# Conv layer norm of a streaming encoder: row sums kept in order of time, high parts written by silu, the output in blocks

## Chip, cores and metric

One NeuronCore of one Trainium2 chip runs the whole step. The metric is the device time of one execution in microseconds, median over runs. Five engines work side by side, each through its own queue in order: PE (matmuls; its weight loads are shown as PEld), DVE, ACT, POOL, and SP, which here only issues DMAs.

## The reference, cut to what matters

Two groups of frames (512 new ones and 64 of running streams, T = 576 columns in all) go through two layers of width 1024. The first layer mixes in time with a Conformer convolution, the second with attention; each is followed by a SwiGLU FFN, and one RMS norm ends the whole.

```python
def conv_module(xn, prefix, w_in, b_in, w_dw, b_dw, ln_g, ln_b, w_out, b_out):
    a, gate = jnp.split(xn @ w_in + b_in, 2, axis=-1)
    u = a * jax.nn.sigmoid(gate)
    u_ext = jnp.concatenate([prefix.astype(u.dtype), u], axis=1)
    y = lax.conv_general_dilated(u_ext, w_dw[:, None, :], ...) + b_dw   # 31 taps, each channel alone
    y = jax.nn.silu(layernorm(y, ln_g, ln_b))
    return y @ w_out + b_out, u_ext[:, -CONV_STATE:]
# trunk: h = h + conv_module(...); h = h + swiglu(rmsnorm(h)); h = h + attention; h = h + swiglu(...)
# return rmsnorm(h, final_norm_g), ...
```

## The kernel before

Activations lie transposed: 8 tiles c = 0..7 of 128 channels by T columns. Every fp32 operand of a product is split into a high part (rounded to fp32r by ACT) and a low part (what is left, by DVE or POOL), and one product is three matmuls: high weights with high activations, high with low, low with high (`mm_ops`, L578, helper line L592). A product of one output tile `wi`, one input tile k and both halves of T is six matmuls.

A planner (class `Plan`, L111) collects operations with a cost, the keys that they read and write, and a few flags. `flush` orders all operations of a section by list scheduling: an engine that comes free takes, among what the planner's own clock has ready, the operation with the longest way to the end (`urgent` ones first), and takes something of lower rank rather than idle. Each engine's queue gets that order. The planner knows the keys only. Waits that come from a new PSUM pool taking over the banks of an old one are not among them; they are added when tiles are placed.

**The convolution.** Tiles 4, 5 and 7 (`POLY`) are convolved on PE in four phases of time (`conv_phases`, L905; products on L923), tiles 0, 1, 2, 3 and 6 (`ROWS`) by taps on DVE (L1046) and on ACT with POOL (L1060, L1063). For the layer norm, sums over channels of y and of y squared are needed. For the row tiles `rows_sums` (L1086) adds each finished y to `ys`, and `square` (L1080) squares it on ACT and adds it to the squares of the first one. Both sums are kept in phases: `in_phases` (L1031) reads a row of time with a stride of four floats. After the last tile (6), `rows_stat` sends both over PE, which sums over partitions (`stat_rows`, L983, helper L979), into one accumulator `cl`. All those matmuls come behind the one that opens the accumulator, the sum `yes` of tiles 4 and 5 that POOL adds up (L1014 to L1026). `warm` matmuls (L775) fill PE's gaps.

**The seam.** From `cl` a short chain on ACT and DVE makes the negative mean `nmp` and the reciprocal deviation `rp`; PE spreads them over all partitions into PSUM (`spread_time`, L1179, helper L1186): `nm` (tag p0), `rt` (tags p5, p4), and a second copy of the mean, `nm2` (tag p1), which ACT copies to SBUF as `nms` for the two tiles that POOL centres. Each tile c is then centred (L1232: DVE reads `nm`; POOL for c = 5 and 7), multiplied by `rt` (L1240), put through silu in place (L1244), copied to its high part (L1250), and the low part is the difference (L1254; POOL for c = 1, 3, 5). Tile 0 goes by halves. Operations on an engine "next" stand for PE's use of the parts, so that the planner sees the order in which they are wanted.

The next section begins with the eight output tiles of w_out (`w_out_tile`, L1799), in the order 0, 4, 1, 5, ... PSUM is a new pool there, and its tags take the eight banks in order of first use: output tile i = 0 (b4, b5) the banks of the tap accumulator, i = 1 (b2, b3) those of p1, i = 2 (b0, b1) those of p0, that is of `nm`. Weights are split in units of 512 columns, two for each output tile. During the convolution four places (w0 to w3) hold the units of i = 0 and 1; the places w4 and w5 open with the next section.

**The end.** `tail` (L1733) finishes the last two output tiles by halves of T; for each half a Newton step (`newton_step`, L681) makes `r`, and the eight tiles of that half are scaled by it: tiles 1, 2, 4, 6 on POOL (`Y_POOL`, L1785; with a scaled copy of h by ACT, L1729), the others on DVE (L1787). Four DMAs of two tiles each (L1795) write that half of `yT`.

Of the kernel before, what the change touches and what calls it, by code (L numbers as in the profile page):

```python
# [75 lines left out]
Y_POOL = (1, 2, 4, 6)  # L76
# [18 lines left out]
WPOOL = {f"{q}{i}" for q in ("w", "wh", "wl") for i in range(4)} | {f"wr{i}" for i in range(3)}  # L95
N_S = 4
# [123 lines left out]
def build(tc, xT, vec, st, stp, bdp, wt, ck, cv, w_in, w_out, gu, down, wk, wv, wq, wo, yT, csp, css, kp, ks, vp, vs):  # L220
# [7 lines left out]
    kpool = ctx.enter_context(tc.tile_pool(name="kpool", bufs=1))  # L228
    dram = ctx.enter_context(tc.tile_pool(name="dram", bufs=1, space=bass.MemoryType.DRAM))
# [86 lines left out]
    def wide(tag):  # L316

        return wpool if tag in WPOOL else cur[0]

# [69 lines left out]
    free = {"wr": [], "w": ["w0", "w1", "w2", "w3"], "S": []}  # L389
# [9 lines left out]
    def place_for(q, ahead):  # L399

        for t in free[q]:
            if not ahead or t in WPOOL:
                free[q].remove(t)
                return t

    def advance():
# [9 lines left out]
        while pos["unit"] < len(units):  # L416
# [4 lines left out]
            tag = place_for("w", u >= eu)  # L421
# [127 lines left out]
    def section():  # L549

        pos["end"] += 1
        hbanks.clear()
        for q in free:
            free[q] = [t for t in free[q] if t in WPOOL]

# [22 lines left out]
    def mm_ops(dst, tag, wi, xkeys, start=True, stop=True, halves=(0, 1), xdeps=None, order=None, keep=False, apart=()):  # L578

        n = len(xkeys)  # L580
        for q, k in enumerate(order or range(n)):
            xk, u = xkeys[k], tile_units[wi][k // 4]

            def f(halves, k=k, xk=xk, u=u, q=q):
# [3 lines left out]
                for j in range(3):  # L588
                    for hf in halves:
# [4 lines left out]
                            start=(start and q == 0 and j == 0), stop=(stop and q == n - 1 and j == 2),  # L594
                        )

            for hs in [(hf,) for hf in halves] if k in apart else [halves]:
                deps = xdeps(xk) if xdeps else [xk + ("h",), xk + ("l",)]
                deps += [xk + (p, 1) for p in "hl"] if 1 in hs else []
# [4 lines left out]
                op("PE", 3 * len(hs) * pe(HA), lambda f=f, hs=hs: f(hs), reads=wkeys(u) + deps, writes=out, group=None if wi < 2 * NC else (wi, halves))  # L604
# [4 lines left out]
    class Norm:  # L609
# [27 lines left out]
        def rstd(self, pair, hf=None, urgent=False):  # L637
# [11 lines left out]
            root(key, tag, halves, rk, urgent)  # L649

    def root(key, tag, halves, rk, urgent=False, wide_=False):
# [27 lines left out]
        newton_step(r[:, sl], lambda: X[("rx",) + key][:, sl], n, xk, rk, urgent)  # L679

    def newton_step(y, x, n, xk, yk, urgent=False):  # L681
# [10 lines left out]

        op("DVE", dve(n), f, reads=yk[:1], writes=[xk], urgent=urgent, port=True)
# [1759 lines left out]
```

## Time and profile before

| | us |
|---|---|
| median of 3 runs (1233.16 to 1234.01) | 1234.01 |
| profiled execution | 1235.98 |
| its span, first to last instruction | 1234.2 |
| PE busy in the span | 1209.6 |
| DVE, ACT, POOL busy | 979.0, 979.4, 772.3 |

Times in the views are microseconds from the first instruction of the profiled execution. "Granted clock" is the share of TensorE's full 2.4 GHz that was granted; 0.50 is 1.2 GHz. In a timeline "x8" counts instructions merged into the row, and square brackets give idle time of that engine before the row and what ended it. An fp32 matmul shows as two records, an fp32r one as one.

### The profile page before, as it was taken

How to read it: one execution, taken by the hardware profiler on the slowest of the kernel's cores; microseconds unless marked ns; L12 is line 12 of the kernel's file. 1: busy time of each engine (PE TensorE's matmuls, PEld its weight loads, DVE VectorE, ACT ScalarE, POOL GpSimd, SP SyncE). 2: the span in 40 equal slices, each digit the busy share in tenths (PEclk: the TensorE clock that was granted, in tenths of full speed). 3: DMA queues.
4: the chain of work that ended last, by engine and by line, in shares of the span. 5: the costliest groups of instructions: out<-in, count | busy, mean ns of one | idle time of the engine just before them, and what ended most of it. 6: DMA issues, size and time to landing. Idle time of an engine off the chain costs nothing.

```text
span 1234.2 us, 24275 instructions
## 1 busy us (share of the span) xinstructions
PE 1209.6 (98%) x8950; PEld 1190.2 (96%) x8950; DVE 979.0 (79%) x1593; ACT 979.4 (79%) x1879; POOL 772.3 (63%) x640
## 2 busy tenths in 40 slices
PE   9999999999999999999999999998999999999996
PEld 8999989999999999999999999998999999999995
DVE  6999976967665669886688999999866666599965
ACT  7988464698887888687678999955988888896873
POOL 1999823479767757855215555554877768676732
PEclk9999989999999999999999999999999999999998
DMA  7333812133242333223372232232232232332222
GB/s 268 87 93 101 260 57 84 52 103 104 70 132 75 101 88 103 87 72 107 112 204 66 49 86 65 53 104 69 69 118 88 86 120 70 103 103 86 86 69 78
DMA packets 46023, 121.10 MB, mean 98 GB/s; under 512 B 8784, under 2 KB 16272, under 8 KB 45904
## 3 DMA queue, kind: packets, MB, share of 16 engines
q1 hardware_dynamic: 45904, 119.56, 32.3%
q8 instruction: 70, 1.15, 0.4%
q14 instruction: 49, 0.40, 0.1%
HBM read 105.18 MB, written 5.70 MB: 90 GB/s over the span
## 4 chain that ended last, share of the span: by engine, by line
PE 80%; DVE 8%; issue 2%; ACT 1%; POOL 0%; DMA 0%; SPq 0%; DVEq 0%; POOLq 0%; ACTq 0%
PE j_A L1411 29%; PE j_B L1411 14%; PE j_C L1411 7%; PE pd L592 7%; PE po L592 4%; PE pq L592 4%; PE b L2189 4%; PE pw L592 2%; PE b L2125 2%; PE b L2217 2%; DVE acc L1046 2%; PE pg L592 1%; PE pv L1940 1%; PE pk L592 1%; DVE wl L520 1%
## 5 line engine op out<-in xcount | busy, mean ns | idle before, releaser
L510 ACT ACTIVATE wh<-wr 128x512 fp32r<-128x512 f32 (+1 forms) x303 | 184.0, 613 | 40.1 <-PE po L592 17.2
L520 DVE TENSOR_TENSOR wl<-wr,hp 128x512 fp32r<-128x512 f32 (+1 forms) x241 | 158.8, 663 | 53.5 <-ACT hp L515 52.0
L520 DVE TENSOR_TENSOR wl<-S,hp 128x512 fp32r<-128x512 f32 x226 | 152.6, 682 | 41.8 <-ACT hp L515 39.0
L510 ACT ACTIVATE wh<-S 128x512 fp32r<-128x512 f32 x228 | 141.1, 626 | 32.6 <-PE pd L592 10.5
L515 ACT ACTIVATE hp<-wr 128x512 fp32r<-128x512 f32 (+1 forms) x241 | 138.9, 578 | 23.9 <-DVE wl L520 20.3
L515 ACT ACTIVATE hp<-S 128x512 fp32r<-128x512 f32 x226 | 133.7, 595 | 12.2 <-POOL S L440 7.1
L440 POOL TENSOR_TENSOR S<-wr,wr 128x512 f32<-128x512 f32 x57 | 76.3, 1338 | 94.6 <-ACT wh L510 38.0
L1063 POOL TENSOR_TENSOR pacc<-pacc,pr 128x608 f32<-128x608 f32 x69 | 109.0, 1595 | 7.3 <-ACT pr L1060 4.1
L476 POOL TENSOR_TENSOR S<-wr,S 128x512 f32<-128x512 f32 x57 | 78.1, 1371 | 31.3 <-DVE wl L520 17.2
L440 POOL TENSOR_TENSOR S<-wr 128x512 f32<-128x512 f32 x57 | 78.2, 1373 | 25.9 <-DVE wl L520 10.1
L440 POOL TENSOR_TENSOR S<-S,wr 128x512 f32<-128x512 f32 x57 | 78.5, 1377 | 12.1 <-DVE wl L520 5.8
L1588 POOL TENSOR_TENSOR a<-a,r 128x576 f32<-128x576 f32 x44 | 67.5, 1536 | 15.7 <-DVE a L1565 14.8
L1588 POOL TENSOR_TENSOR t<-t,r 128x576 f32<-128x576 f32 x44 | 66.5, 1515 | 10.0 <-ACT t L1559 8.7
L592 PE MATMUL pd<-ap,wh 128*128 128x288 f32 x384 | 66.0, 294 | 0.0
L1046 DVE SCALAR_TENSOR_TENSOR acc<-u,vecs,acc 128x608 f32<-128x608 f32 x76 | 64.7, 851 | 1.0
L1060 ACT ACTIVATE pr<-u,vecs 128x608 f32<-128x608 f32 x69 | 54.2, 798 | 8.2 <-POOL pacc L1063 7.9
L520 DVE TENSOR_TENSOR wl<-wr,wh 128x512 fp32r<-128x512 f32 x62 | 49.7, 813 | 7.8 <-ACT wh L510 7.7
L592 PEld LDWEIGHTS pd<-ap,wh 128*128 128x128 f32 x384 | 55.9, 188 | 0.0
L1594 DVE TENSOR_TENSOR a<-a,t 128x576 f32<-128x576 f32 x44 | 48.1, 1094 | 8.1 <-ACT t L1592 7.8
L1559 ACT ACTIVATE t<-j_A 128x288 f32<-128x288 f32 x84 | 34.0, 407 | 22.8 <-PE j_A L1411 22.2
L1680 DVE TENSOR_TENSOR h<-j_A,h 128x288 f32<-128x288 f32 x60 | 27.2, 455 | 19.6 <-PE j_A L1411 19.4
L1565 DVE TENSOR_TENSOR t<-j_C,t 128x288 f32<-128x288 f32 x42 | 19.2, 457 | 29.1 <-PE j_C L1411 28.8
(856 smaller groups left out, 4523.7 us busy)
## 6 DMA issues: line engine op xcount, KB each, us to landing
wr<-gu SPq DMA_DIRECT2D x88, 512.0 KB, 3.6
wr<-down SPq DMA_DIRECT2D x32, 512.0 KB, 4.1
wr<-w_in SPq DMA_DIRECT2D x15, 512.0 KB, 3.9
wm<-wt SPq DMA_DIRECT2D x12, 576.0 KB, 5.4
wr<-down SPq DMA_DIRECT2D x16, 384.0 KB, 3.1
qd<-qd SPq DMA_DIRECT2D x21, 256.0 KB, 3.2
wr<-w_out SPq DMA_DIRECT2D x8, 512.0 KB, 3.6
wr<-wq SPq DMA_DIRECT2D x8, 512.0 KB, 3.9
```

The costliest lines, as they stand in the source:

```text
L440: eng(e).tensor_tensor(t[:, :n], x[1](), y[1](), op=ALU.subtract if sub else ALU.add)
L476: eng(e).tensor_tensor(v[:, :n], X[("raw", i0)][:, n : 2 * n], v[:, :n], op=ALU.subtract)
L510: nc.scalar.activation(X[("w", u)][0][:, :n], get(), AF.Copy)
L515: nc.scalar.activation(t[:, :n], get(), AF.Copy)
L520: eng(le).tensor_tensor(b[:, :n], get(), a.bitcast(F32)[:, :n], op=ALU.subtract)
L592: nc.tensor.matmul(o[hf], (hi, hi, lo)[j][:, s], (xh, xl, xh)[j], start=(start and q == 0 and j == 0), stop=(stop and q == n - 1 and j == 2),)
L1046: nc.vector.scalar_tensor_tensor(dst, src, wt_, dst if i else X[("kneg",)], op0=ALU.mult, op1=ALU.add)
L1060: nc.scalar.activation(tile(("pr", c, i), f"pr{m}", (P, YW)), src, AF.Copy, scale=wt)
L1063: nc.gpsimd.tensor_tensor(X[("pacc", c)], X[("pacc", c)], X[("pr", c, i)], op=ALU.add)
L1411: nc.tensor.matmul(out, a[:, s], b, start=(start and q == 0 and i == 0), stop=(q == len(ops_) - 1 and i == 2), skip_group_check=True,)
L1588: nc.gpsimd.tensor_tensor(X[k], X[k], r, op=ALU.mult)
L2189: nc.tensor.matmul(zz()[:, a : a + n], X[("trir",) if same else ("oner",)], X[key][:, x, c : c + n], start=False, stop=(i == len(mms) - 1) ...
```

## The change

- `ys` and the squares are kept in order of time; PE now reads them with the stride of four floats (`stat_rows`). The sum of tiles 0 to 3 goes to PE after tile 3, and tile 6 goes to PE by itself instead of being added to `ys`.
- The square of tile 6 is made by halves, one on ACT and one on DVE.
- `nm2` is gone; ACT makes `nms` from `nm`, after tile 0 has been centred.
- silu writes the high part itself (rounded on output), and a second silu in place makes the full value from which the low part is taken. For the first three output tiles PE takes, for each input tile, the two matmuls with its high part and then the one with the low part of the tile before (`lag`).
- A fifth place w4 is open during the convolution, for the first unit of output tile i = 2 only.
- In the tail, `newton_step` also writes its result to a PSUM bank, and DVE's scalings read it there; POOL keeps tiles 2 and 4 only. `yT` has the shape (2, 4, 128, 576), so that each DMA writes one contiguous block; the host puts it back in order.

```diff
-Y_POOL = (1, 2, 4, 6)
+Y_POOL = (2, 4)
...
+WPOOL2 = {"w4", "wh4", "wl4"}
...
-    def place_for(q, ahead):
+    def place_for(q, ahead, third=False):
         for t in free[q]:
-            if not ahead or t in WPOOL:
+            if t in WPOOL or (third if t in WPOOL2 and not pos["end"] else not ahead):
...
-            tag = place_for("w", u >= eu)
+            tag = place_for("w", u >= eu, u >= eu + 4)
...
-        for q, k in enumerate(order or range(n)):
+        steps = [(q, k, (0, 1, 2)) for q, k in enumerate(order or range(n))]
+        if lag:
+            steps = [x for c in range(n + 1) for x in ((c, c, (0, 2)), (c - 1, c - 1, (1,))) if 0 <= x[0] < n]
+        for q, k, js in steps:
...
-                for j in range(3):
+                for j in js:
...
+        def b():
+            o = tile(("rb", bank), bank, (P, 512), pool=pp)[:, :n]
+            nc.vector.scalar_tensor_tensor(o, x(), 1.5, y, op0=ALU.add, op1=ALU.mult)
...
+        if bank:
+            op("DVE", dve(n, True), b, reads=[xk] + yk[:1], writes=[bank], urgent=urgent, port=True)
         op("DVE", dve(n, True), s, reads=[xk], writes=yk, urgent=urgent, port=True)
...
+            if q and c == ROWS[-1]:
+                nc.vector.tensor_tensor(o, x, x, op=ALU.mult)
+            else:
+                nc.scalar.activation(o, x, AF.Square)
...
+        if c == ROWS[-1]:
+            op("ACT", act(HY, False), lambda: f(0), reads=[("y", c)], writes=[(tag, 0)], urgent=True)
+            op("DVE", dve(YW - HY), lambda: f(1), reads=[("y", c)], writes=[(tag, 1)], urgent=True, port=True)
...
         if c in KN[2:]:
-            add(("ys",), "ys", ("y", c), ("y", c), True)
+            add(("ys",), "ys", ("y", c), ("y", c))
...
-            add(("ys",), "ys", ("y", c), ("y", c), True)
+            if c != ROWS[-1]:
+                add(("ys",), "ys", ("y", c), ("y", c))
             square(c)
...
-        stat_rows(lambda: X[("ys",)], "ys", 0)
-        stat_rows(lambda: X[("sq", a)], "ysq0", 1)
+        if c == ROWS[-2]:
+            stat_rows(lambda: in_phases(X[("ys",)]), ["ys"], 0)
+        if c == ROWS[-1]:
+            stat_rows(lambda: in_phases(X[("y", c)]), [("y", c)], 0)
+            stat_rows(lambda: in_phases(X[("sq", a)]), by_part("ysq0"), 1)
...
-    spread_time(("nm2",), "nmp", "p1")
-    op("ACT", act(T, False), lambda: nc.scalar.activation(tile(("nms",), "kneg", (P, YW))[:, :T], X[("nm2",)][:, O0 : O0 + T], AF.Copy), reads=both("p1"), writes=["kneg"])
...
-            nc.scalar.activation(part(X[("zt", c)][0], hs), part(X[("zf", c)], hs), AF.Copy)
+            nc.scalar.activation(part(X[("zt", c)][0], hs), part(X[("zf", c)], hs), AF.Silu, scale=col(V_LNG + c), bias=col(V_LNB + c))
...
+        if not c:
+            op("ACT", act(T, False), lambda: nc.scalar.activation(tile(("nms",), "kneg", (P, YW))[:, :T], X[("nm",)][:, O0 : O0 + T], AF.Copy), reads=NT + [zt], writes=["kneg"])
...
-            nrm.rstd(("b6", "b7"), hf, True)
+            nrm.rstd(("b6", "b7"), hf, True, ("b5", "b2")[hf])
...
-                            nc.vector.scalar_tensor_tensor(o, h[c][:, sl], col(V_FIN + c), r[:, sl], op0=ALU.mult, op1=ALU.mult)
+                            nc.vector.scalar_tensor_tensor(o, h[c][:, sl], col(V_FIN + c), X[rb][:, : sl.stop - sl.start], op0=ALU.mult, op1=ALU.mult)
...
-                    nc.sync.dma_start(yT[2 * q : 2 * q + 2, :, sl].rearrange("c p t -> p c t"), X[yk])
+                    nc.sync.dma_start(yT[hf, q], X[yk].rearrange("p c t -> p (c t)"))
...
+        if i < 3:
+            mm_ops(k, tag, wi, [("z", c) for c in range(NC)], apart=() if i else (0,), lag=True)
```

## Rows read from the trace of the kernel before

**Rows 1.** The page: busy time, share of the span and instructions of each engine.

```profile
PE 1209.6 (98%) x8950; PEld 1190.2 (96%) x8950; DVE 979.0 (79%) x1593; ACT 979.4 (79%) x1879; POOL 772.3 (63%) x640
```

**Rows 2.** Windows: stretch, length, busy per engine (instructions), granted clock, DMA share, GB/s.

```profile
160.00:170.00 10.00, 7.44 (x50) 6.74 (x49) 9.85 (x26) 7.88 (x13) 5.39 (x5) 0.84 0.17 52
...
300.00:500.00 200.00, 200.00 (x1510) 200.00 (x1509) 140.13 (x221) 167.01 (x341) 147.19 (x113) 1.00 0.32 95
...
168.00:170.00 2.00, 2.00 (x9) 2.00 (x10) 2.00 (x6) 1.45 (x3) 2.00 (x2) 0.50 0.00 0
...
174.00:176.00 2.00, 2.00 (x17) 2.00 (x16) 2.00 (x3) 1.97 (x5) 0.46 (x1) 1.00 0.00 0
```

**Rows 3.** Waits of PE from 110 to 180 us: total, times, longest.

```profile
PE po L592 <- POOL zl L1254: 2.0, 1, 2.0
...
PE po L592 <- ACT nms L1215: 0.5, 1, 0.5
```

**Rows 4.** Timeline of the seam: start, length, engine, line, operation, count, [idle before].

```profile
160.77 0.63 ACT L1244 ACTIVATE zf<-zf,vecs 128x288 f32<-128x288 f32 x1 [1.89 <-DVE zf L1240]
...
160.97 1.95 PE L1186 MATMUL nm<-nmp,row_of 128*128 128x72 f32 x16
...
162.72 0.38 PE L592 MATMUL po<-zh,wh 128*128 128x288 f32 x1
...
166.30 1.92 DVE L1232 TENSOR_TENSOR zf<-y,nm 128x512 f32<-128x512 f32 x4
...
167.90 0.85 PE L592 MATMUL po<-zl,wh 128*128 128x288 f32 x2 [1.99 <-POOL zl L1254]
```

**Rows 5.** ACT's silu and copy in the seam: shortest, median, longest in ns.

```profile
L1244 ACT ACTIVATE zf<-zf,vecs x9: 627/856/870, 160.8 to 173.4; 128x576 f32<-128x576 f32 x7, 128x288 f32<-128x288 f32 x2
...
L1250 ACT ACTIVATE zh<-zf x9: 444/667/689, 161.4 to 174.3; 128x576 fp32r<-128x576 f32 x7, 128x288 fp32r<-128x288 f32 x2
```

**Rows 6.** Timeline of DVE in the convolution: row sums, squares and a weight's low part.

```profile
75.27 2.00 DVE L1093 TENSOR_TENSOR ys<-y,y 128x608 f32<-128x608 f32 x1
...
86.05 1.75 DVE L1134 SCALAR_TENSOR_TENSOR ys<-kneg,ys 128x608 f32<-128x608 f32 x1
...
125.65 0.68 DVE L520 TENSOR_TENSOR wl<-wr,hp 128x512 fp32r<-128x512 f32 x1
...
132.02 2.56 DVE L1076 TENSOR_TENSOR ys<-ys,y 128x608 f32<-128x608 f32 x1
...
135.27 1.30 DVE L1076 TENSOR_TENSOR sq<-sq,sq 128x608 f32<-128x608 f32 x1
```

**Rows 7.** Timeline of the convolution's end: phase products, sums and the first reader.

```profile
141.96 7.25 PE L923 MATMUL py<-vt,wm 128*128 128x152 f32 x54 [0.51 <-DVE ye L933]
...
149.04 0.45 PE L979 MATMUL cl<-yes,sum_of 128*128 128x152 f32 x2
...
152.05 1.32 ACT L1082 ACTIVATE sq<-y 128x608 f32<-128x608 f32 x1 [0.60 <-DVE y L1070]
...
152.15 1.26 DVE L1076 TENSOR_TENSOR ys<-ys,y 128x608 f32<-128x608 f32 x1
...
153.40 0.79 DVE L1076 TENSOR_TENSOR sq<-sq,sq 128x608 f32<-128x608 f32 x1
...
154.61 1.20 PE L979 MATMUL cl<-sq,sum_to 128*128 128x152 f32 x8
...
155.84 0.30 ACT L1192 ACTIVATE vs<-cl 128x152 f32<-128x152 f32 x1 [2.48 <-PE cl L979]
```

**Rows 8.** Timeline of the last half of the output.

```profile
1220.09 3.81 POOL L1785 TENSOR_TENSOR yo<-hg,r 128x288 f32<-128x288 f32 x4 [8.60 <-DVE r L691]
...
1222.20 0.45 DVE L1760 TENSOR_TENSOR h<-pd,h 128x288 f32<-128x288 f32 x1
...
1226.41 0.46 DVE L691 SCALAR_TENSOR_TENSOR r<-rx_cs_fin,r 128x288 f32<-128x288 f32 x1
...
1226.91 4.04 DVE L1787 SCALAR_TENSOR_TENSOR yo<-h,vecs,r 128x288 f32<-128x288 f32 x4
```

More of the change, by code (lines that the diff above doesn't have):

```diff
@@ L316, in wide @@
     def wide(tag):
-        return wpool if tag in WPOOL else cur[0]
+        return wpool if tag in WPOOL else wpool2 if tag in WPOOL2 and pos["end"] < 2 else cur[0]
     vecs = base.tile([P, NV], F32, name="vecs")
@@ L388, in build @@
     lo_eng = ["DVE"]
-    free = {"wr": [], "w": ["w0", "w1", "w2", "w3"], "S": []}
+    free = {"wr": [], "w": [f"w{i}" for i in range(5)], "S": []}
     pos = {"src": 3, "unit": 0, "tile": 0, "end": 0}
@@ L553, in section @@
         for q in free:
-            free[q] = [t for t in free[q] if t in WPOOL]
+            free[q] = [t for t in free[q] if t in WPOOL or (t in WPOOL2 and pos["end"] < 2)]
     def by_part(tag):
@@ L593, in f @@
                             o[hf], (hi, hi, lo)[j][:, s], (xh, xl, xh)[j],
[L594 removed]
+                            start=(start and q == 0 and j == 0), stop=(stop and q == n - 1 and j == js[-1] and (not lag or j == 1)),
                         )
             for hs in [(hf,) for hf in halves] if k in apart else [halves]:
[L598 to L599 removed]
+                parts = "hl" if len(js) == 3 else "h" if 0 in js else "l"
+                deps = xdeps(xk) if xdeps else [xk + (p,) for p in parts]
+                deps += [xk + (p, 1) for p in parts] if 1 in hs else []
                 if isinstance(tag, tuple):
@@ L1133, in sums_less_mean @@
         op("ACT", act(YW), kneg, reads=[kt], writes=["kneg"])
-        op("DVE", dve(YW, True), lambda: nc.vector.scalar_tensor_tensor(X[("ys",)], in_phases(X[("kneg",)]), float(n), X[("ys",)], op0=ALU.mult, op1=ALU.add), reads=["kneg"], writes=["ys"], port=True)
+        op("DVE", dve(YW, True), lambda: nc.vector.scalar_tensor_tensor(X[("ys",)], X[("kneg",)], float(n), X[("ys",)], op0=ALU.mult, op1=ALU.add), reads=["kneg"], writes=["ys"], port=True)
     def project(c):
@@ L1450, in ffn @@
         free["wr"].append("wr3")
-        free["w"] += [f"w{i}" for i in range(4, N_W)]
+        free["w"] += [f"w{i}" for i in range(4 if l else 5, N_W)]
         free["S"] += [f"S{i}" for i in range(N_S)]
@@ L1808, in build @@
     ffn(0, w_out_tile, V_KVG, nkv, XT, [])
+    w_pool2.close()
     att_pool = ExitStack()
```

81 lines of the change are left out of this document (42 added, 39 removed).

## Prediction

> **What bounds the kernel now.** First I read the busy shares: PE is busy for 98% of the span [rows 1], and in the middle of an FFN it runs without a gap, 1510 matmuls in 200 us or 0.1325 us each [rows 2]. A change gains only where PE stands still, runs slow, or isn't the last to finish. Next come the windows by stage. The stretch that this change touches, 160 to 170 us, has PE at 7.44 of 10 us and a mean granted clock of 0.84; in 168 to 170 us the clock is 0.50 (1.2 GHz), in 174 to 176 it is 1.00 again (2.4 GHz) [rows 2]. The list of waits names two causes: w_out's products (`po`) waited 2.0 us for the low part of tile 1, made by POOL, and 0.5 us for ACT's copy `nms` [rows 3]. The timeline gives the rest: the first product starts at 162.72, just behind the second copy of the mean on PE (160.97 plus 1.95), though tile 0's high part could have been there earlier; PE stops for 1.99 us and goes on at 167.90 [rows 4]. From there to the tail PE is nearly closed, so what the seam gains or loses is carried to the end one for one. Before the seam DVE is the engine without gaps; at the very end it is DVE again [rows 8].
>
> **Part A, the sums.** Before, ACT's first reader of the sums starts at 155.84, behind the squares' matmuls at 154.61 plus 1.20 [rows 7].
> On DVE, three row sums with strided operands took 2.00, 1.75 and 2.56 us [rows 6]. The contiguous add of the same size, beside the same POOL work, took 1.30. The three save 0.70 + 0.45 + 1.26 = 2.4. The new early weight unit adds one low part, 0.68 [rows 6], if the planner puts it ahead of the last tile, as it does with the four units that it splits early now; I take that, and 0 as the other end. So tile 6 is ready about 1.7 us earlier, at 150.3 instead of 152.0 (the square that waits for it starts at 152.05) [rows 7]. Behind it stood 1.26 and 0.79 on DVE; now stand half a square (about 0.46, the size of the 288-column operations [rows 8]) and 0.79. With 1.20 for the matmuls and small waits DVE's way ends at about 152.9.
> PE's way is longer. The phase products end at 149.21 (141.96 plus 7.25, in which no gap is left but the 0.51 before it). Behind them come all sums, since the first of them needs POOL's `yes`, at 149.04 [rows 7]: 2 + 2 + 8 records for these and for the squares of the first phase tiles and the row sums, 8 for tile 7, 8 for tile 6, 8 for the squares. That is 36 at 7.25/54 = 0.134 us, 4.8 us, and with a start at 148.7 to 149.2 an end at 153.5 to 154.0. Against 155.81 that is a gain of 1.8 to 2.3; I take 2.0.
> That holds if PE reads a stride of four floats as fast as a packed row, and no row shows PE doing it. DVE's strided add took 1.26 where the packed one took 0.79 [rows 7]: 0.47 us over 608 elements, 0.77 ns each, which on PE would be 0.12 us a record and 2.8 us over the 24 strided ones. The bounds are thus 0 and 2.8; a gain has no reason. Nearest is PE itself: it takes 0.88 ns a column in fp32 (0.134/152) and 0.46 ns in fp32r (0.1325/288) [rows 2, 7], so in fp32 some 0.42 of the 0.77 may be hidden. I take the rest, 0.35 ns a column, 0.053 us a record, 1.3 us. Part A: 2.0 - 1.3 = +0.7, ends -0.8 and +2.0.
> The Trainium skill, page "SBUF — State Buffer", section "Door 1: The DMA port swizzle", speaks against this step: the memory has lines of 16 bytes, and an access that goes to a new line each time pays. Here every float read lies in a line of its own. DVE's two rows agree; for PE no row of this case decides, and by that rule alone the dear end, the second rival, would be right.
>
> **Part B, the seam.** Taken out: 16 records of `nm2` (1.95 us) on PE, and ACT's copy to the high part (0.667 us), which a second silu (0.856) replaces behind the first [rows 5]. ACT then has 1.71 us a tile instead of 1.52, so tile 7 comes no earlier; the high part of tile 0 comes at 160.77 + 0.63 = 161.40, and PE can start at 161.45 instead of 162.72. The wait for a low part made by POOL falls away as the first in line, since its matmul comes a tile later. The copy `nms` moves into ACT's idle 1.89 us ahead of its first silu [rows 4] and costs nothing there; in the worst case it holds that silu up by its own length, 0.63.
> What is late next? From 161.45 PE has tile 0 for the output tiles i = 0 and 1: about nine matmuls until 163.5. Then tile 0's last low part or tile 1's high part (silu of a whole tile, 0.856) is still missing, and the planner takes what it holds ready: output tile i = 2, whose first weights now lie in w4. But its accumulator gets the banks of `nm`, and those come free only when DVE has centred its last tile. That wait is not in the planner's keys. The row for it: i = 1 waited 0.5 us for `nms`, the last reader of the banks that it took over [rows 3]. DVE ended its last centring at 166.30 + 1.92 = 168.2 [rows 4], and nothing in the change takes work off DVE ahead of it. PE's queue is in order, so i = 0 and 1 stand behind that matmul, and PE stops from 163.5 to 168.2. Before, it went on at 167.90 with 14 matmuls done (between 162.72 and there); now at 168.2 with 9. The loss is 0.3 + 5 x 0.1325 = 1.0. The clock falls in this gap as it did in the shorter one, and comes back after the same 5 us of work, at no difference. Part B: -1.0. Bounds: if all centrings go ahead of the other work, DVE is through at about 166.2 and B is +1.0; if multiplications and low parts go ahead of them, about 170 and -2.8.
>
> **Part C, the tail.** DVE's four scalings took 4.04 us, 1.01 each, while POOL ran its own; but the add at 1222.20, which reads PSUM, took 0.45 in the middle of POOL's 3.81 [rows 8]. With `r` in PSUM six scalings at 0.46 and a gap of 0.03 are 2.94. The one more write (0.49) goes ahead of them. From 1226.87, where `r` was ready, to the last scaling: 3.43 instead of 4.08, a gain of 0.65. POOL's two (about 0.95 each) end earlier. In the first half, the add at 1222.20 stood behind slow scalings; with short ones I give it 0.35. One block for each write instead of two half rows: 0 to 0.2, taken as 0.1. Part C: +1.1, bounds 0.4 and 1.5.
>
> **Sum.** 0.7 - 1.0 + 1.1 = 0.8 us. The span of the profiled execution, 1234.2, becomes 1233.4, and that execution 1235.2 (1.8 lie around the span). It is 2.0 above the median shown; taken off that median, 1234.01 - 0.8 = **1233.2**.
>
> **Rivals.**
> First, i = 2 doesn't block (the planner finds other work, or the banks fall otherwise). Before, the 96 matmuls of i = 0 and 1 ended at about 181.2: from 167.90 on 22 at half clock in 5.3 us, then 60 in 8.0. Now they would begin at 161.45 and need 12.7 us and about 1.4 of small gaps, but not before the last low part, near 176.2: 5.0 us instead of -1.0. Then 0.7 + 5.0 + 1.1 gives 1227.2. For it: PE would have a third tile as filling. Against it: the wait of 0.5 us in [rows 3], and i = 2 gets the one pair of banks with readers until 168.2.
> Second, and slower: PE pays the full stride. Then A is 2.0 - 2.8 = -0.8 and the sum -0.8 - 1.0 + 1.1 = -0.7, 1234.7. The place is the sums between 148.7 and 157 us; it decides from 2.1/24 = 0.09 us more a record on, 0.22 instead of 0.134. For it: DVE's 0.77 ns. Against it: the spare time of an fp32 column.
> Third, other orders: the planner lays out the convolution and all later sections anew; any of them may open or close a wait of a microsecond or two.
>
> **How the numbers follow.** Forecast 0.45, no block 0.20, full stride 0.27, other orders 0.08. The forecast's own range, from the bounds of A and B, is 1230.5 to 1235.5. The whole range, **1226.8 to 1236.8**, leaves out the lower part of the first rival and late banks with the full stride, less than 2 in 10. 0.2% is 2.5 us, about what a measurement of this kernel can tell from no change. Faster by more (under 1231.5): nearly all of the first rival and the third of the forecast with early banks or a free stride, **0.37**. Slower by more (over 1236.5): late banks with the full or a part stride, and bad orders, **0.14**. Within: **0.49**.
>
> **What would show it.** A: strided sum records of 0.15 to 0.22 us and the first reader of `cl` at about 155.1. B: no `nm2`, the first `po` about 1.3 us nearer to the first silu, then one wait of over 4 us that ends with DVE's last L1232, and the clock at 0.50 behind it. Wrong, if PE has no gap above 1 us in the seam and keeps 1.00 (then 1227), or if the records of the sums take 0.25. C: scalings at 0.46, the last of them 3.4 us behind `r`. It would be wrong altogether if a later section shows a new wait of PE of several microseconds.

## The result, and the profile after

| | before | after |
|---|---|---|
| median, us (6 runs each) | 1234.01 (1233.16 to 1235.65) | 1239.15 (1238.78 to 1240.99) |
| profiled execution | 1235.98 | 1239.61 |
| its span | 1234.2 | 1237.9 |

The ratio is 1.0043, with an interval of 1.003 to 1.0056: the change costs 5.1 us, and the forecast of 1233.2 and its range missed. Executions of one kernel lie up to 5 us apart, so terms below a microsecond are read from intervals inside the traces, not from times. A trace is of one execution, and its intervals vary too (e2 below, by 0.8 us).

The span is cut at three events that both kernels have: ACT's first reader of the sums, the first matmul of the next norm's sum (`cs_f`; 216 of w_out's matmuls lie ahead of it in both), and the first step of the root in the tail (`rx_cs_fin`). The two of before that aren't in the rows above, by the timeline (start, length, engine, line, operation, count):

```profile
197.52 1.14 PE L708 MATMUL cs_f<-ss_f,ones 128*128 128x288 f32 x4
...
1217.56 0.46 DVE L666 TENSOR_SCALAR rx_cs_fin<-cs_fin 128x288 f32<-128x288 f32 x1 [2.15 <-ACT r L670]
```

and after:

```profile
157.21 0.30 ACT L1218 ACTIVATE vs<-cl 128x152 f32<-128x152 f32 x1 [5.47 <-PE cl L994]
...
202.56 1.14 PE L723 MATMUL cs_f<-ss_f,ones 128*128 128x288 f32 x4
...
1222.48 0.46 DVE L675 TENSOR_SCALAR rx_cs_fin<-cs_fin 128x288 f32<-128x288 f32 x1 [2.15 <-ACT r L679]
```

| stretch | before | after | gain | predicted |
|---|---|---|---|---|
| start to reader (A) | 155.84 | 157.21 | -1.37 | +0.7 |
| reader to `cs_f` (B) | 41.68 | 45.35 | -3.67 | -1.0 |
| `cs_f` to the tail's root | 1020.04 | 1019.92 | +0.1 | 0 |
| root to the end (C) | 16.64 | 15.42 | +1.22 | +1.1 |
| span | 1234.2 | 1237.9 | -3.7 | +0.8 |

The spans give 3.7 of the 5.1 us. The other 1.4 or so is that before's profiled execution was 2.0 above its median and after's only 0.5. In 95 more executions of before, made beside the experiments, the time goes with the mean granted clock of the execution: the 27 at 0.997 have a median of 1233.17, the 17 at 0.994 one of 1235.31. Before's trace is at 0.994 and longer than all but 3 of the 95, so a gain that is read against it can be too large by up to 1.8 us, and a loss too small.

**A.** PE's timeline at the convolution's end, after; [rows 7] has the packed records of before:

```profile
149.24 2.32 PE L994 MATMUL cl<-ys,sum_to 128*128 128x152 f32 x8
...
152.43 2.32 PE L994 MATMUL cl<-y,sum_to 128*128 128x152 f32 x8
154.57 2.34 PE L994 MATMUL cl<-sq,sum_to 128*128 128x152 f32 x8
```

Eight records read with the stride are busy for 2.32 us, where packed ones took 1.20; from start to start they take 2.14 (152.43 to 154.57), 0.27 each. PE has no wait in this stretch: the squares were there at 152.88 and PE came to them at 154.57.

**B.** The list of PE's waits from 110 to 180 us (total, times, longest), after, and then the windows; [rows 3] and [rows 2] answer to them:

```profile
PE po L600 <- DVE zf L1255: 6.8, 1, 6.8
...
PE po L600 <- ACT zh L1273: 0.5, 1, 0.5
```

```profile
160.00:170.00 10.00, 5.18 (x43) 4.72 (x41) 8.56 (x23) 7.92 (x12) 6.63 (x6) 0.87 0.16 52
170.00:180.00 10.00, 7.49 (x39) 7.49 (x40) 6.99 (x14) 6.95 (x10) 1.53 (x2) 0.62 0.08 15
```

The waits of 2.0 for POOL's low part and of 0.5 for `nms` are gone. In their place stand one of 6.8 us, which ends with DVE's centring, and one of 0.5 for the second half of tile 0's high part (`zh`). PE's timeline and then DVE's, to be laid beside [rows 4]:

```profile
157.01 2.39 PE L790 MATMUL warm<-ones 128*128 128x128 f32 x20
159.24 1.90 PE L1212 MATMUL nm<-nmp,row_of 128*128 128x72 f32 x16
...
162.77 1.10 PE L790 MATMUL warm<-ones 128*128 128x128 f32 x8
163.62 0.38 PE L600 MATMUL po<-zh,wh 128*128 128x288 f32 x1
...
172.51 0.85 PE L600 MATMUL po<-zh,wh 128*128 128x288 f32 x2 [6.78 <-DVE zf L1255]
```

```profile
162.77 0.82 DVE L1255 TENSOR_TENSOR zf<-y,nm 128x512 f32<-128x512 f32 x2 [0.24 <-ACT nms L1286]
...
169.53 1.53 DVE L1263 TENSOR_TENSOR zf<-rt,zf 128x288 f32<-128x288 f32 x4
170.99 0.73 DVE L1277 TENSOR_TENSOR zl<-zf,zh 128x576 fp32r<-128x576 f32 x1
171.65 0.80 DVE L1255 TENSOR_TENSOR zf<-y,nm 128x512 f32<-128x512 f32 x2
```

PE issues 8 matmuls and stands still from 165.7 to 172.51, where DVE's last centring (171.65 plus 0.80) frees the banks of `nm` for output tile i = 2. Ahead of that centring DVE did four multiplications (two tiles, by halves) and a whole low part. Behind the stop two records of po take 0.48 us from start to start, until 177.5; from there 0.26, as elsewhere.

**C.** DVE's timeline of the last half of the output, after ([rows 8]):

```profile
1231.32 0.46 DVE L700 SCALAR_TENSOR_TENSOR r<-rx_cs_fin,r 128x288 f32<-128x288 f32 x1
1231.69 2.63 DVE L1815 SCALAR_TENSOR_TENSOR yo<-h,vecs,rb_b 128x288 f32<-128x288 f32 x6
```

Six scalings in 2.63 us, 0.44 each, where four took 4.04.

### The profile page after: what moved, and what is told of

It is laid out like the page before. It is cut to its first block, busy times and chain, and to the rows that moved or that the text cites. A ratio compares the mean times of both kernels' runs of the same rounds, so it can differ in the third digit from the quotient of the medians.

```text
span 1237.9 us, 24260 instructions
## 1 busy us (share of the span) xinstructions
PE 1211.4 (98%) x8942; PEld 1191.4 (96%) x8942; DVE 978.9 (79%) x1599; ACT 975.8 (79%) x1878; POOL 761.2 (61%) x636
## 4 chain that ended last, share of the span: by engine, by line
PE 84%; DVE 8%; ACT 3%; POOL 2%; DMA 1%; issue 1%; SPq 0%; DVEq 0%; POOLq 0%; ACTq 0%
PE j_A L1439 29%; PE j_B L1439 14%; PE pd L600 7%; PE j_C L1439 7%; PE po L600 4%; PE pq L600 4%; PE b L2222 4%; PE pg L600 2%; PE pw L600 2%; PE b L2158 2%; PE b L2250 2%; POOL pacc L1078 2%; DVE acc L1061 1%; DVE wl L524 1%; PE pv L1973 1%
## 5 line engine op out<-in xcount | busy, mean ns | idle before, releaser
L1616 POOL TENSOR_TENSOR a<-a,r 128x576 f32<-128x576 f32 x44 | 67.1, 1526 | 15.4 <-DVE a L1593 14.5
L2124 POOL TENSOR_TENSOR e<-t,e 128x512 fp32r<-128x512 f32 (+1 forms) x20 | 27.0, 1351 | 23.1 <-DVE e L2120 12.3
```

The lines of the kernel that those rows point to most:

```text
L1616: nc.gpsimd.tensor_tensor(X[k], X[k], r, op=ALU.mult)
```

## The experiments

Theory: the records pay the whole stride (A), the third output tile blocks PE's queue behind a late centring (B), and the tail gains (C). The kernels take these apart. Their marks, from the timelines (us); each ratio goes against runs of before made beside it, with medians of 1234.11 to 1234.43 (1234.01 for after):

| kernel | reader | reader to `cs_f` | span | median | ratio to before |
|---|---|---|---|---|---|
| before | 155.84 | 41.68 | 1234.2 | 1234.01 | |
| after | 157.21 | 45.35 | 1237.9 | 1239.15 | 1.0043 [1.003, 1.0056] |
| e1 | 156.00 | 41.75 | 1232.9 | 1233.61 | 0.9995 [0.9986, 1.0004] |
| e2 | 158.30 | 40.84 | 1235.5 | 1236.99 | 1.0022 [1.0013, 1.0031] |
| e3 | 157.29 | 38.75 | 1231.1 | 1233.46 | 0.9996 [0.9987, 1.0005] |
| e4 | 158.78 | 40.76 | 1233.9 | 1236.42 | 1.0016 [1.0007, 1.0025] |
| e5 | 156.52 | 38.73 | 1230.7 | 1233.97 | 0.9997 [0.9988, 1.0005] |
| e6 | 157.44 | 38.71 | 1230.7 | 1232.54 | 0.9989 [0.998, 0.9997] |
| e7 | 159.70 | 38.18 | 1232.8 | 1235.58 | 1.0007 [0.9999, 1.0016] |
| e8 | 160.61 | 39.18 | 1235.0 | 1236.16 | 1.0016 [1.0007, 1.0025] |
| e9 | 154.53 | 38.12 | 1229.0 | 1230.20 | 0.9966 [0.9953, 0.9978] |
| e10 | 156.90 | 38.72 | 1230.6 | 1232.65 | 0.9985 [0.9976, 0.9994] |
| e11 | 157.84 | 42.63 | 1235.4 | 1236.58 | 1.0019 [1.001, 1.0027] |
| e12 | 157.16 | 43.25 | 1235.5 | 1237.72 | 1.0029 [1.002, 1.0038] |

### The three parts

**e1, the tail alone**, in the kernel before:

```diff
-Y_POOL = (1, 2, 4, 6)
+Y_POOL = (2, 4)
...
-            nrm.rstd(("b6", "b7"), hf, True)
+            nrm.rstd(("b6", "b7"), hf, True, ("b5", "b2")[hf])
...
-                    nc.sync.dma_start(yT[2 * q : 2 * q + 2, :, sl].rearrange("c p t -> p c t"), X[yk])
+                    nc.sync.dma_start(yT[hf, q], X[yk].rearrange("p c t -> p (c t)"))
```

> The kernel before with part C alone (r for DVE in PSUM, POOL with two tiles instead of four, output in blocks); convolution and seam are those of before. Theory (part C is worth what the two traces show): in the profile after, the way from the first root step of the first half (1222.48) to the end of the span (1237.9) is 15.4 us, in that of before (1217.56 to 1234.2) 16.6. So this kernel takes 1.2 us less than before: 1232.8, and its last way is 15.4 us. Rival (the shorter tail is only the other phase of the later sections in the changed kernel, or one block for each write gives back what DVE gains): 1234.0, and a last way of 16.3 us or more.

From the root's first step (1217.50) to the end are 15.4 us, as in after, against 16.64. The trace bears out 1.2 us; the time, 0.5 us under the runs of before beside it with an interval from -1.7 to +0.5, can't tell it from nothing.

**e2, the stride alone**, in the kernel before: the same 16 row-sum records, read with the stride, so that the floats come in another order.

```diff
-(lambda j=j: x()[:, j, :])
+(lambda j=j: x().rearrange("p j n -> p (j n)").rearrange("p (n j) -> p j n", j=Q)[:, j, :])
```

> The kernel before, in which the two sums over the row tiles (ys and sq, 16 records on PE) read the same packed tiles at a stride of four floats. The sums go to wrong times for it, so the normalised values are not the reference's; all instructions, sizes and orders are those of before. Theory (TensorE pays for the stride, whatever wrote the tile): eight records take 2.3 us instead of 1.2 to 1.3, the second eight start where the first end, so that the first reader of the sums starts at 157.9 instead of 155.84, and all behind it is 2.1 us later: 1236.1. Rival (the long records of the changed kernel come from something else, such as tiles just written or two engines reading them): 1.2 to 1.3 us for eight, 1234.0. In between, at 0.2 us a record: 1235.0.

The sums' end in e2's timeline, PE and ACT:

```profile
153.70 2.40 PE L979 MATMUL cl<-ys,sum_to 128*128 128x152 f32 x8 [0.23 <-DVE ys L1076]
...
155.92 2.34 PE L979 MATMUL cl<-sq,sum_to 128*128 128x152 f32 x8
...
158.30 0.30 ACT L1192 ACTIVATE vs<-cl 128x152 f32<-128x152 f32 x1 [4.71 <-PE cl L979]
```

The reader comes 2.46 us later, 0.23 of it because the row sums begin later (153.70, before 153.47). The rest over 16 records is 0.14 us each. The full stride is paid.

Only 1.6 of the 2.46 us are left at `cs_f`, though the instructions between are those of before and PE has the same waits of 2.0 and 0.5. The clock differs. Windows of before and then of e2:

```profile
160.00:170.00 10.00, 7.44 (x50) 6.74 (x49) 9.85 (x26) 7.88 (x13) 5.39 (x5) 0.84 0.17 52
170.00:180.00 10.00, 10.00 (x64) 10.00 (x64) 7.78 (x14) 7.51 (x12) 3.00 (x3) 0.81 0.16 52
```

```profile
160.00:170.00 10.00, 7.81 (x63) 7.11 (x61) 9.02 (x25) 7.29 (x12) 2.93 (x3) 1.00 0.17 54
170.00:180.00 10.00, 9.59 (x59) 9.24 (x60) 9.36 (x17) 8.78 (x14) 5.48 (x5) 0.83 0.00 0
```

In e2 the clock falls 1.4 us behind the end of the stop of 1.99 us (PE restarts at 170.36; 0.90 in 171 to 172, then 0.50). In before it falls within that stop (0.95 in 166 to 167, then 0.50; PE restarts at 167.90), so that more matmuls run at half speed. What the seam of before costs is thus not the same in each execution.

**e3, the third tile behind the centrings**, in the kernel after: the planner learns that i = 2 needs all of DVE's centrings.

```diff
-            op("DVE", 0.82, f, reads=NT + ys, writes=[zt], urgent=c == 0)
+            op("DVE", 0.82, f, reads=NT + ys, writes=[zt, ("ctr", c)], urgent=c == 0)
...
-            mm_ops(..., apart=() if i else (0,), lag=True)
+            mm_ops(..., apart=() if i else (0,), lag=True, more=[("ctr", c) for c in range(NC) if c not in ZF_POOL] if i == 2 else [])
```

> The changed kernel, in which the third output tile of the projection (i = 2) may stand in PE's queue only behind the planner's time of DVE's last centring; the orders of DVE, ACT and POOL in the seam are unchanged. Theory (the wait of 6.8 us is the third tile's banks, and the first two tiles stand behind it in the queue for nothing): no wait of PE above 1.2 us in the seam, PE goes on at 166.1 with tile 1's high part and follows the parts as they come; from 163.6 to 177.5 it does about 100 matmuls instead of 47, so that the sums cs_f (263 matmuls behind the start) come at 199 instead of 202.56: 1235.6 (1235 to 1237). Rival (the second silu and the late low parts keep PE waiting with or without the third tile): waits of PE of 5 us and more in several pieces, cs_f at 202 and 1238.5 to 1239.5.

Waits of PE from 110 to 180 us and windows, e3:

```profile
PE po L600 <- ACT zh L1273: 2.4, 3, 1.5
...
```

```profile
160.00:170.00 10.00, 7.61 (x58) 6.91 (x58) 8.56 (x24) 7.91 (x12) 6.56 (x6) 1.00 0.19 52
170.00:180.00 10.00, 9.95 (x75) 9.71 (x74) 9.06 (x19) 8.74 (x13) 1.66 (x2) 1.00 0.07 11
```

This one key takes 5.7 us off the median of after: the wait of 6.8 is gone, the clock stays at 1.00. The long stop and its clock are thus the whole of B's loss, and more. `cs_f` stands at 196.04 and the time is 1233.46, both better than expected (199, and 1235 to 1237): the expectation had counted 263 matmuls ahead of `cs_f` instead of 216, and 100 of them done by 177.5 where it was 77. Reader to `cs_f` is 2.9 shorter than before, where the first rival gave 5.0.

**e4, another way round the banks**, in the kernel after: DVE centres tiles 1 to 4 and 6 from `nms` in SBUF, so that nothing but tile 0 reads `nm`.

```diff
-                m = X[("nms",)][:, a:b] if c in ZF_POOL else X[("nm",)][:, O0 + a : O0 + b]
+                m = X[("nms",)][:, a:b] if c else X[("nm",)][:, O0 + a : O0 + b]
...
-            op("DVE", 0.82, f, reads=NT + ys, writes=[zt], urgent=c == 0)
+            op("DVE", 0.82, f, reads=(["kneg"] if c else NT) + ys, writes=[zt], urgent=c == 0)
```

> The changed kernel, in which DVE centres the tiles behind the first one with ACT's copy of the mean (nms, in SBUF) as POOL does, so that the banks of nm come free at 162.8 instead of 172.45. Theory: the third tile is free to run with the first two, 12 matmuls (1.6 us) for each tile of z that comes every 1.7 us; no wait of PE above 1.2 us, clock at 1.00 or near it, cs_f at 195 to 197 instead of 202.56, less what DVE's centring costs more from SBUF while POOL works (0.2 to 0.5 us a tile, four of them): 1233.5 (1232 to 1235). Rival (ACT and DVE bound the seam, the third tile gives PE nothing that it could use): no better than the third tile last, 1236.

DVE and POOL in the timeline of e4:

```profile
163.67 2.16 DVE L1255 TENSOR_TENSOR zf<-y,nms 128x512 f32<-128x512 f32 x2 [0.24 <-ACT nms L1286]
...
163.72 4.35 POOL L1255 TENSOR_TENSOR zf<-y,nms 128x512 f32<-128x512 f32 x4 [14.48 <-ACT nms L1286]
...
169.61 1.55 DVE L1255 TENSOR_TENSOR zf<-y,nms 128x512 f32<-128x512 f32 x4
...
171.09 2.83 POOL L1277 TENSOR_TENSOR zl<-zf,zh 128x576 fp32r<-128x576 f32 x2 [3.02 <-DVE zf L1255]
```

The expectation missed. i = 2 no longer blocks, but DVE's centring of one tile from SBUF (two instructions) beside POOL's takes 2.16 us, where it took 0.82 with `nm` in PSUM (after, 162.77). While POOL stands idle, from 168.1 to 171.1, two tiles from SBUF take 1.55, no more than from PSUM (1.54 before, at 163.38): it is POOL's work beside it that costs. The same happens to a half low part at 166.13: 1.73 instead of 0.45. The interval, 40.76, is 2.0 above e3's, and ahead of the seam the newly laid convolution waits 1.7 us for the weights of the phase products, so that the reader is at 158.78.

**e5, the seam alone**, in the kernel before: part B with e3's key, without the sums and the tail.

```diff
-    spread_time(("nm2",), "nmp", "p1")
...
-            nc.scalar.activation(part(X[("zt", c)][0], hs), part(X[("zf", c)], hs), AF.Copy)
+            nc.scalar.activation(part(X[("zt", c)][0], hs), part(X[("zf", c)], hs), AF.Silu, scale=col(V_LNG + c), bias=col(V_LNB + c))
...
+            mm_ops(..., lag=True, more=[("ctr", c) for c in range(NC) if c not in ZF_POOL] if i == 2 else [])
```

> The kernel before with part B alone (high parts straight from silu, low parts a tile later, a fifth weight unit for the third output tile), and with the third tile behind DVE's last centring in PE's queue; sums and tail are those of before. Theory (part B is a gain as soon as the third tile blocks nobody): first reader of the sums at 155.8 as before, no wait of PE above 1.6 us behind the first product, clock 1.00 in 160 to 180; the sums cs_f come 2.5 to 3 us before the 197.5 of the kernel before, and the time is 1231.3 (1230.5 to 1232.5). Rival (ACT's 1.71 us a tile instead of 1.52, and the first silu behind nms, eat what the early high parts give): cs_f at 196.5 or later and 1233.5 or more.

The interval is 38.73, as in e3: against before's trace, B without the block is 2.9 shorter whatever stands ahead of it. By an estimate 2.4 of that is the clock, which stays at 1.00 in the seam of e3 and e5 while before does 22 matmuls at 0.24 us instead of 0.1325, and the other 0.5 is the earlier first product. The times don't bear out the whole 2.9. The profiled execution of e5, 1232.38, lies in the expected range, but it was the shortest of twelve, and the median missed by 2.7 us. The medians of e3, e5 and e6 lie 0.7, 0.4 and 1.8 below those of before; with their own A and C taken off, some 1 to 2 us are left for B (an estimate, each with an interval of about 1 us either way). Part of the 2.9 is thus the one long execution that before's trace is of. The new layout also has PE wait 2.3 us for the phase products' evacuation, and the reader comes 0.7 later.

### The sums

**e6, the sums as before**, with e3's key:

```diff
-            stat_rows(lambda: in_phases(X[("y", c)]), [("y", c)], 0)
-            stat_rows(lambda: in_phases(X[("sq", a)]), by_part("ysq0"), 1)
...
+        stat_rows(lambda: X[("ys",)], "ys", 0)
+        stat_rows(lambda: X[("sq", a)], "ysq0", 1)
```

> The changed kernel with the third tile last (as in e3), and with part A undone: row sums and squares packed by phases again, the last square whole on ACT. Theory (strided reads on PE made part A a loss): eight records of the row sums in 1.2 to 1.3 us instead of 2.3, first reader at 155.8 instead of 157.29, all behind it 1.4 us earlier than in e3: 1232.0, or 1231 if e3's own profiled execution (1232.8) is the better base. Rival (DVE's longer strided adds come back in full, so that the order of the sums is as good either way): first reader at 157 and the time of e3, 1233.5.

e6, the reader by the timeline, and a window around 145 us:

```profile
157.44 0.30 ACT L1207 ACTIVATE vs<-cl 128x152 f32<-128x152 f32 x1 [2.00 <-PE cl L994]
```

```profile
144.00:146.00 2.00, 2.00 (x9) 2.00 (x9) 1.93 (x3) 0.00 (x0) 2.00 (x2) 0.50 1.02 365
```

The reader was expected at 155.8 and came at 157.44. PE had stopped 2.94 us for a phase evacuation, and the clock was 0.50 behind that. The time, 1232.54, is near the 1232.0 expected by luck: what was to make it didn't come. The planner lays the convolution out anew when its sums change, so this run doesn't measure A; e9 does.

**e9, the stride for nothing**: e3, but the strided records read packed (the sums then mix the times; the work is otherwise the same).

```diff
-        stat([(..., (lambda j=j: x()[:, j, :])) for j in range(Q)], deps, i)
+        stat([(..., (lambda j=j: x()[:, j * QW : j * QW + QW])) for j in range(Q)], deps, i)
...
-            stat_rows(lambda: in_phases(X[("y", c)]), [("y", c)], 0)
+            stat_rows(lambda: X[("y", c)], [("y", c)], 0)
```

> The changed kernel with the third tile last (e3), in which the 24 strided records of the sums read the same tiles packed, 152 floats in a row: the sums go to wrong times, so the normalised values are not the reference's; orders, sizes and all else are those of e3. It gives part A without the stride on PE. Theory (the stride alone made part A a loss): eight records take 1.2 us instead of 2.3, the way of PE ends with the squares' add on DVE (152.9) and 1.2 plus 0.3 us of records: first reader at 154.6 to 154.9 instead of 157.29, 1.0 us earlier than the kernel before had it, all behind it as much earlier, and 1231.0 against 1233.5 of e3. Rival (the order of the sums itself puts them late): first reader at 156 or later.

The same stretch in e9's timeline:

```profile
152.00 1.20 PE L994 MATMUL cl<-y,sum_to 128*128 128x152 f32 x8
153.03 1.20 PE L994 MATMUL cl<-sq,sum_to 128*128 128x152 f32 x8
...
154.53 0.30 ACT L1218 ACTIVATE vs<-cl 128x152 f32<-128x152 f32 x1 [2.80 <-PE cl L994]
```

The reader comes 2.76 us ahead of e3's (157.29), with nothing else changed in the plan: that is the price of 24 strided records here. At 0.14 each they cost 3.3; the difference is mostly that with packed records PE has to stop for `ye` (ahead of 151.64), which the strided ones hide. Against before (155.84) the new order of the sums would gain 1.3 without it. The time (of five runs) is 1230.20, where 1231.0 was expected.

**e7, packed by ACT**: e3 with squares written in phases and a packed copy of `ys` on ACT, which takes `kneg`'s place. **e8** is e7 with fewer warm matmuls in the seam and `nms` ahead of tile 0's centring.

```diff
+            op("ACT", act(YW, False), lambda: nc.scalar.activation(tile(("ysp",), "kneg", (P, Q, QW)), in_phases(X[("ys",)]), AF.Copy), reads=["ys"], writes=["kneg"])
-            stat_rows(lambda: in_phases(X[("ys",)]), ["ys"], 0)
+            stat_rows(lambda: X[("ysp",)], ["kneg"], 0)
```
```diff
-N_WARM = (10, 14)
+N_WARM = (10, 8)
...
-    reads=NT + [zt], writes=["kneg"])
+    reads=NT, writes=["kneg"], urgent=True)
```

> The changed kernel with the third tile last, and with ACT, which has 8.8 of 10 us idle between 140 and 150, packing the row sums by phases in one copy ahead of tile 6 and writing the squares packed; DVE's adds stay contiguous; of the 24 strided records on PE only tile 6's own 8 are left. Theory: 16 records at 0.13 instead of 0.27 are 2.2 us of PE's way; the first reader at 155.2 instead of 157.29 and 1231.4. Rival (the half of the last square that DVE now writes from a strided read, and ACT's packing, are late, DVE's way ends last): first reader at 156 or later, 1232.3 or more.

> As e7, and the copy of the mean (nms) ahead of the first centring instead of behind it, and 8 warm-up matmuls instead of 14 between the sums and the projection. In the changed kernel 20 warm records held the spread of the mean up from 158.8 to 159.24, 8 more stood ahead of the first product (from 162.77, the high part was ready at 163.26), and nms stood ahead of the first silu. Theory: these give 0.4, 0.3 and 0.1 us, 0.8 together, and the clock stays at 1.00: first product 5.4 us behind the first reader of the sums instead of 6.4, and 1230.6. Rival (the spread waits for the mean itself, and the clock falls with less work ahead of the projection): the time of e7 or above it, and a granted clock under 1.00 in 160 to 170.

Both missed. The packed records take 1.20 per eight, but y of tile 6 is ready at 155.9 instead of 150.7, and the reader comes at 159.70. The likely cause is the copy's place in `kneg`, which DVE's taps read too: with a buffer of its own (e10) y is ready at 150.67, but e10 also leaves the squares as they were, so this isn't shown. In e8 `nm` waits 0.65 us for `nmp` itself, so that fewer warm matmuls bring little there: the first po is 5.7 us behind the reader, against 6.1 in e7 and 6.4 in after. The granted clock is 0.83 from 150 to 160 us, behind a wait of 1.96 us for `ye`, and 0.93 in the next ten.

**e10, the row sums packed**: e3 with that copy in a buffer of its own.

```diff
+            op("ACT", act(YW, False), lambda: nc.scalar.activation(tile(("ysp",), "ysp", (P, Q, QW)), in_phases(X[("ys",)]), AF.Copy), reads=["ys"], writes=["ysp"])
-            stat_rows(lambda: in_phases(X[("ys",)]), ["ys"], 0)
+            stat_rows(lambda: X[("ysp",)], ["ysp"], 0)
```

> As e3, with the sum of the row tiles packed by phases by one copy on ACT, which is idle there, into a buffer of its own: 8 of the 24 strided records become packed ones, the rest stays. Theory: 1.1 us of PE's way goes, the row sums end at 150.3 instead of 151.5; the sums of tile 6 (ready at 150.7) and of the squares (152.9) follow without a gap; first reader at 156.2 instead of 157.29, and 1232.4 (1 us less than e3). Rival (tile 6 and the squares end last anyway, the row sums run in a pause of PE): first reader at 157.0 or later, 1233.4.

The same stretch in e10's timeline:

```profile
148.34 1.20 PE L994 MATMUL cl<-ysp,sum_to 128*128 128x152 f32 x8
...
151.64 0.53 PE L994 MATMUL cl<-ye,sum_of 128*128 128x152 f32 x2 [1.33 <-DVE ye L1017]
...
154.15 2.34 PE L994 MATMUL cl<-sq,sum_to 128*128 128x152 f32 x8
...
156.31 0.56 PE L994 MATMUL cl<-sq,sum_of 128*128 128x152 f32 x2
...
156.90 0.30 ACT L1219 ACTIVATE vs<-cl 128x152 f32<-128x152 f32 x1 [5.17 <-PE cl L994]
```

```profile
154.00:155.00 1.00, 1.00 (x6) 1.00 (x5) 0.00 (x0) 0.00 (x0) 0.00 (x0) 0.50 0.20 28
155.00:156.00 1.00, 1.00 (x5) 1.00 (x4) 0.00 (x0) 0.00 (x0) 0.00 (x0) 0.50 0.51 128
```

Eight records are cheap again, but the time becomes a wait of 1.33 for `ye`, which stands in PE's queue ahead of tile 6's records though y is ready at 150.67. The reader gains 0.4 on e3, not 1.1. The eight strided records at 154.15 take 2.16 us from start to start at a granted clock of 0.50, as they take 2.14 in after at 1.00: it is the stride that sets their time, not PE's clock. At 0.9985 [0.9976, 0.9994] this version is ahead of the kernel before and of the change.

### Inside the seam

**e11, centring first**, in the kernel after: all of DVE's centrings are marked urgent, so that the planner takes them as soon as they can run.

```diff
-            op("DVE", 0.82, f, reads=NT + ys, writes=[zt], urgent=c == 0)
+            op("DVE", 0.82, f, reads=NT + ys, writes=[zt], urgent=True)
```

> The changed kernel with the third tile left where it blocks, and all of DVE's centrings ahead of its multiplications and low parts. Theory (the stop of PE ends with DVE's last centring, wherever that stands): the last centring ends at 167.5 to 168.5 instead of 172.45, and the wait of the third tile with it, about 2 us long instead of 6.8; the parts of z come later for it (silu waits for multiplications that now stand behind the centrings), so that a second wait of 1 to 2 us for the high part of tile 1 follows; from the first reader to the sums cs_f 41.5 to 43 us instead of 45.35, and 1236 to 1237.5. Rival (it is not the banks of the mean that hold the third tile): a wait of 6 us or more that ends after 171.

DVE's last centrings and PE's restart in e11's timeline:

```profile
167.56 1.90 DVE L1255 TENSOR_TENSOR zf<-y,nm 128x512 f32<-128x512 f32 x4
...
169.51 0.53 PE L600 MATMUL po<-zh,wh 128*128 128x288 f32 x2 [3.15 <-DVE zf L1255]
```

The last centring ends at 169.46, and PE goes on at 169.51. That end is 11.6 us behind the reader, against 15.2 in after and 12.4 before, and the interval to `cs_f` is 42.63: B is then -0.95. The stop is 3.15 us long, not 2, since the last centring ends a microsecond later than expected. PE's restart follows the last centring wherever that is put, so the banks are the cause.

**e12, the stop filled**, in the kernel after: 46 more matmuls of tile 0 ahead of the third tile's first one (they add to output tile 0).

```diff
+                if fill and q == 0 and 0 in js:
+                    for r_ in range(46):
+                        nc.tensor.matmul(full(X[fill[0]])[r_ % 2], ..., start=False, stop=False, skip_group_check=True)
```

> The changed kernel, in which 46 more matmuls (the first tile's high parts again, into the first output tile, which so gets products too many and is not the reference's) stand in PE's queue right ahead of the third tile's first one, where PE would stop: 46 at 0.1325 are 6.1 of the 6.8 us. The third tile still waits until 172.5. Theory (the stop costs twice: its own length, and then 5 us at the lower clock level): the wait is 0.7 us instead of 6.8, the granted clock in 170 to 180 us is 1.00 instead of 0.62, the products behind 172.5 run at 0.1325 us each, cs_f comes 2.5 us earlier, at 200.0, and the time is 1236.7. Rival (the clock falls there for another reason): 0.6 again, cs_f at 202.5 and 1239.2.

PE's timeline and a window of e12:

```profile
165.53 6.28 PE L599 MATMUL po<-zh,wh 128*128 128x288 f32 x46
172.59 0.54 PE L604 MATMUL po<-zh,wh 128*128 128x288 f32 x2 [0.79 <-DVE zf L1259]
```

```profile
170.00:180.00 10.00, 9.21 (x69) 8.98 (x68) 7.10 (x15) 6.95 (x10) 1.56 (x2) 1.00 0.08 18
```

The useful work goes on at the same moment (172.59 against 172.51) and the clock is 1.00 instead of 0.62; `cs_f` comes at 200.41 instead of 202.56. The stop of 6.8 us thus costs 2.1 us more by the lower clock behind it.

## Why the prediction was wrong, step by step

**Part A, the order of the sums: right, a little large.** Predicted 2.0, measured 1.3 (e9 against before). y of tile 6 was ready at 150.67, not at 150.3; the sums began at 149.14, the upper end of the stretch given; a wait of 0.27 for `ye` came in between, and ACT's reader starts 0.2 behind the place where a next record would start, which the sum left out.

**Part A, the price of the stride: a failed step.** "... so in fp32 some 0.42 of the 0.77 may be hidden. I take the rest, 0.35 ns a column, 0.053 us a record, 1.3 us." e2 and after give 0.14 us a record, and e9 gives 2.76 us in all; the dear end, from DVE's 0.77 ns, was 0.12 and 2.8. PE hides nothing of it: the prediction had read what an fp32 column takes longer than an fp32r one as spare time. That the total is so near the dear end's 2.8 is luck in part, since each record cost more and a wait for `ye` hid some. The second rival, with its deciding point at 0.09, was the case, and so part A is 1.3 - 2.8. The rule of the Trainium skill ("SBUF — State Buffer", "Door 1: The DMA port swizzle") is that each access that crosses to a new 16-byte line pays. The strided records agree with it: 0.27 against 0.13 us for 152 columns.

**Part B, the mechanism: right.** i = 2 took the banks of `nm`, PE's queue stood behind it in order, and it did 8 matmuls before that where nine were expected. e3 removes the stop by telling the planner, e11 moves it with the last centring.

**Part B, the start: gain 0.47 instead of 1.27.** Reader to first po went from 6.88 to 6.41 us. PE holds 20 warm matmuls in one block where before it had 16, so `nm` starts at 159.24 though `nmp` is ready at 158.73 (0.4). `nms` holds ACT's first silu up by 0.1. The other 0.3 is eight new warm matmuls (162.77) ahead of the first po, whose high part is ready at 163.26. The prediction's "costs nothing there" was said of ACT's queue, and nothing of PE's own.

**Part B, the restart: the other failed step, and the one that cost most.** "DVE ended its last centring at 166.30 + 1.92 = 168.2 [rows 4], and nothing in the change takes work off DVE ahead of it." It put work ahead of it. From its first centring to the end of its last DVE took 8.84 us before and 11.27 after: four multiplications (1.53), a low part (0.73) and a wait of 0.24 for `nms`. With 0.44 from the later `nm`, the last centring ends 2.9 later, counted from the reader (12.4 to 15.2), and PE's restart follows it. The bound of 170 had this mechanism in mind, and was 0.9 us short of it: its -2.8 stands against -3.67. With the centrings early, as in e11, B is -0.95. That this is the forecast's own term is luck: e11's first product comes 0.8 later behind the reader than forecast, its stop ends 0.7 earlier, and another of 0.84 for a high part follows (171.15).

**The clock.** "At no difference" held for these two traces: PE worked at 0.50 from 172.5 to 177.5 after, from 167.9 to about 173.5 before [rows 2]. e12 prices it at 2.1 us after. Before pays some 2.4 in its trace (the estimate under e5), less in e2, and what it pays in a median execution isn't shown.

**Part C: right, with two terms that cancel.** 1.22 against 1.1, and e1 has the same by itself. Scalings with `r` in PSUM start 0.44 apart. From the root to the end of the last scaling are 11.84 us after (1222.48 to 1234.32) and 13.39 before (1217.56 to 1230.95), a gain of 1.55 where 1.0 was forecast; but from there to the end of the span are 3.6 instead of 3.3, so the blocks, which were to gain 0.1, brought nothing.

**Sum and rivals.** Second rival and late banks came together, -0.8 and -2.8 by the text's own bounds; with C that made 1236.5, at the range's end. Part A came out 0.6 below its bound, B 0.9, and the median lies 1.4 further than the spans differ. What was wrong besides the sizes was the small chance that each dear end got, though each had a row for it. The first rival would not have been worth 5.0 but 2.9 at most (e3, e5, e6 alike, against before's trace): its start gains 0.8 less, and PE waits 2.4 us for high parts where 1.4 was allowed.

Open is where before's profiled execution lost its 2 us against the median. Its low mean clock, and e2's seam, 0.84 shorter, point to the clock behind PE's stops; no trace of a median execution shows it.

## What to carry to other kernels

A planner that orders an in-order queue must know what frees a bank: one key (e3) was worth 5.7 us here, more than all that the change meant to gain. When work is reordered, follow the instruction that releases the next resource through its engine's whole queue, since its old time is no bound. A stride that one engine pays for by the element is to be charged in full to another until a row shows it hidden. And a gain read from two traces is to be set against the medians: the 2.9 us of the seam here were 1 to 2 in the times.

## What the runs showed of the hardware

- PE's fp32 moving operand with a stride of four floats: 0.27 us for 152 columns, against 0.13 packed (after, e2, e9), 0.9 ns more a column. DVE's adds paid 0.77 ns an element [rows 7]. At a granted clock of 0.50 the strided record still takes 0.27 (e10).
- DVE's operation with both operands in SBUF beside POOL's with the same kind: the centring of one tile takes 2.16 us, against 0.82 with one operand in PSUM, and 0.78 with both in SBUF while POOL is idle (e4). The Trainium skill, "SBUF — State Buffer", "Who interferes with whom", says that a DVE instruction with two SBUF inputs contends with a GpSimd instruction that reads SBUF; e4 agrees.
- The length of a stop alone doesn't tell whether the clock falls: it stayed at 1.00 behind 1.48 us in e3 and 2.3 in e5, and was 0.53 in 153 to 156 us behind 1.33 in e10 and 0.50 behind 1.99 before, 2.94 in e6 and 6.78 after. Behind the same 1.99 in e2 it stayed at 1.00 for another 1.4 us.
